# Combine placed one unit later, the first decays in single banks, silu behind the next query's copy, the last products of up and the first banks of down reordered

## The chip, the cores and the metric

The kernel runs on one core of a Trainium2 chip. The metric is the device time of the whole kernel in microseconds (us). The time before is the median of three executions. Its five engines, by the names used here, are TensorE (PE, with its weight loads listed apart as PEld), VectorE (DVE), ScalarE (ACT), GpSimd (POOL) and SyncE (SP), which issues the transfers.

## The reference

Two residual layers over a sequence of 1024 tokens with 1024 features. Layer 0 mixes tokens with a gated MLP and with dilated attention, layer 1 with chunked gated linear attention (GLA); each layer ends with a gated MLP with a causal convolution. Cut to what the change touches:

```python
def even_mixer(h, w_in, a_ln_g, a_ln_b, a_ws, a_bs, q_g, k_g, w_out):
    ...
    for window, dilation in B_BRANCHES:
        o_r, l_r = dilated_branch(qh, kh, vh, window, dilation)
        outs.append(o_r)
        lses.append(l_r)
    wts = jax.nn.softmax(jnp.stack(lses), axis=0)
    o = jnp.einsum('rbhs,rbhsc->bhsc', wts, jnp.stack(outs))
    ...

def gla_mixer(h, w_in, w_a2, b_a, head_g, w_out):
    ...
    log_a = jax.nn.log_sigmoid((ga @ w_a2 + b_a).astype(jnp.float32)) / C_TAU
    o = gla_chunked(heads(q, C_DK) * (C_DK ** -0.5), heads(k, C_DK), heads(v, C_DV),
                    heads(log_a, C_DK))
    o = rms_norm(o, head_g)
    o = o.transpose(0, 2, 1, 3).reshape(Bn, S, hv) * jax.nn.silu(r.astype(jnp.float32))
    return o.astype(h.dtype) @ w_out

def conv_ffn(h, w_gate, w_up, conv_w, conv_b, w_down):
    g = causal_dwconv(h @ w_gate, conv_w, conv_b)
    return (jax.nn.silu(g) * (h @ w_up)) @ w_down
```

## The kernel before

All large products are made in float32 split into a high and a low part, so that each product of two tiles is three matmuls. A split is a copy to the high part (mostly ACT, line 100) and a subtraction for the low part (DVE, line 101). Independent instructions are put in order by the framework's scheduler when the program is built; an instruction that the program hands to `keep_in_program_order` stays where the code has it on its engine. Each engine runs its instructions strictly in that order.

**Attention of layer 0** (`project`, `unit`, `dilated`, `combine`) goes over four pairs of heads. For a pair, `project` makes eight token tiles n: a projection into one of two banks named pj (line 190), a norm of queries and keys (the tile qn, line 768, which is the last reader of pj and lets the bank go), a split of qn on POOL and DVE (qs, ks), transposes, and one `unit` of banded attention (scores sc, mask and sum sm on DVE at line 711, transposes pP, output po). `dilated` then does the strided branch and writes its result to memory (od); it is loaded back in two halves as the tiles on. `combine` weighs the two branches of one half g: a minimum cM (line 838, kept in program order), exponentials cE, and in `combined` the denominators cD and the products at lines 849 to 857, one of them on POOL. While the next pair is projected, the combine of the pair before runs behind two of its units, through the argument `then`.

**GLA of layer 1.** `values` makes the value projections (pv, tag mm, three tiles of two banks each) with the preparation of the decays of head 0 inserted (`decays(0, ...)`, whose two products are the tiles pla, read by ACT and by DVE at line 1083). Then the streams q0, r0, q1, r1, ... follow, one for queries and keys of a head and one for its gate. Each is two of 128-wide row blocks made with seven products numbered 1 to 7 instead of eight; products 1, 6, 7, 4 share a bank B, 5 and 3 share C, 2 has A. The bank of each B product is read before the next one may start: line 1059 copies product 6 (ACT), line 1063 adds product 7 (DVE). After a gate stream, silu is applied to its result `or` in two halves (line 1168, ACT, with a load of the function table ahead of them), and it is written to memory; `core` runs the chunked recurrence (pat, pog, og).

**The MLP.** `ffn_up` works in streams as well, a gate stream g and an up stream u for every two row blocks; the products come as 5, 6, 2, 7, then 1 of the next stream, then 4 and 3. Line 302 copies product 7 (ACT, s1), line 305 product 4. `ffn_down` accumulates over all row blocks into banks named pd: B (two double tiles, pdB and pdC), O (a double tile pdO and the single ones pdP and pdQ). In layer 1 the first product goes to B.

Of the kernel before, what the change touches and what calls it, by code (L numbers as in the profile page):

```python
# [9 lines left out]
F32 = mybir.dt.float32  # L10
# [3 lines left out]
AF = mybir.ActivationFunctionType  # L14
# [5 lines left out]
P = 128  # L20
# [8 lines left out]
HEADS_C = 4  # L29
EPS = 1e-6  # L30
BIG = 1e30
HALVES = ((0, slice(0, 512)), (1, slice(512, 1024)))
# [7 lines left out]
PASSES = ((0, 0), (0, 1), (1, 0))  # L40
# [15 lines left out]
def trunk(ctx: ExitStack, tc: tile.TileContext, a, out):  # L56
# [181 lines left out]
    def ffn_up(l, T3, ps, pool, norm_end):  # L238
# [6 lines left out]
        def stream(kind, f):  # L245
# [31 lines left out]

            def step(p):
                if p not in made:
# [8 lines left out]
                for j in range(4):  # L288
                    for ii, jj in PASSES:
                        T.matmul(o, L[ii][:, j * P : j * P + P], right[p][:, jj, j, :], skip_group_check=more,  # L290
                                 start=(not more and j == 0 and (ii, jj) == PASSES[0]),
                                 stop=(j == 3 and (ii, jj) == PASSES[-1]))
                if p == 1:
# [66 lines left out]
        for i, (kind, f) in enumerate(todo):  # L360
            step, out, _ = cur
            early = (1, 2) if i < 2 else (1,)
            for p in (5, 6, 2, 7):
                if p not in early:
                    step(p)
            if 0 < i < len(todo) - 1:
                nxt = stream(*todo[i + 1])
                nxt[0](1)
            step(4)
            step(3)  # L370
            if kind == "g":
                ts = conv(f, out)
            else:
                for j in range(2):
                    V.tensor_mul(ts[j], ts[j], out[:, j, :])
                down_acts(f, *ts)
                down_weights(f)
            cur = nxt


    def ffn_down(l, ps, pool, xs, final):
# [12 lines left out]
        def mm(o, t, side, start, stop, more):  # L394
            L, R = side
            for ii, jj in PASSES:
# [297 lines left out]
    def attention(ps, at, av, pq, pq0, par0, wx, wq0, gqk, masks, rest, gm_open):  # L694
# [42 lines left out]
        def outputs(name):  # L737
            return (at.tile([P, 4, 132], F32, tag="ot", name="ot" + name, bufs=5),
                    ps.tile([P, 4, P], F32, tag="po", name="po" + name))

        def project(p, ws=None, then=None, early=None):
# [35 lines left out]
            for n in range(NT):  # L777
# [83 lines left out]
        for p in range(PAIRS):  # L861
# [11 lines left out]
            def then(g):  # L873
                weights(g)()
# [23 lines left out]
    def gla(ps, narrow, gl, T3, rl):  # L898
# [43 lines left out]
        def values():  # L942

            for i, (col, step, w) in enumerate(((0, 272, 1), (256, 256, 2), (512, 512, 1))):
# [6 lines left out]
                for m in sorted(range(NT // (2 * w)), key=lambda m: 2 * w * m < 4):  # L951
# [191 lines left out]

        cur = begin(*todo[0])
        cur[0](1)
        for i, (kind, h) in enumerate(todo):
            step, out = cur
            for p in (5, 6, 2, 7) if i + 1 < len(todo) else (6, 2, 7):
                step(p)
            if i + 1 < len(todo):  # L1150
                nxt = begin(*todo[i + 1])
                nxt[0](1)
# [4 lines left out]
            if kind == "q":  # L1157
# [6 lines left out]
                if h + 1 < HEADS_C:  # L1164
                    dc = decays(h + 1)
            else:
                for _, c in HALVES:
                    A.activation(out[:, :, c], out[:, :, c], AF.Silu)
# [177 lines left out]
```

## Time and profile before

| what | value |
|---|---|
| executions | 2165.72, 2161.59, 2159.29 us, median 2161.59 us |
| profiled execution | 2167.37 us, of which the span is 2165.6 us |
| PE busy | 2134.3 us of the span (99%) |
| DVE, ACT, POOL busy | 71%, 48%, 23% of the span |
| mean granted clock of PE | 0.996 |

The profile shows one execution, the profiled one, which is 5.8 us above the median of the others. In the rows, the first number is the start in us from the beginning of the span, the second the duration in us, then come the engine, the line of the code, the operation, what it writes and reads, shape and count of like instructions in a row; a bracket at the end is the idle time of that engine ahead of it and what ended it. Rows of the list of waits give total, times and the longest, in us. Rows by windows give for a stretch of time the busy time of each engine, then the granted clock of PE as a share of full speed, the share of transfers and their rate.

### The profile page before, as it was taken

To read this page: it belongs to the slowest core of one execution; us is meant where nothing else is said; L and a number is where in the kernel's file an instruction comes from. 1 tells how busy PE (TensorE), PEld (TensorE's weight loads), DVE (VectorE), ACT (ScalarE), POOL (GpSimd) and SP (SyncE) were. 2 spreads that over 40 slices of the span, in tenths; PEclk is the share of its full clock that TensorE was granted. 3 is DMA by queue.
4 is the path that set the end of the run, shared out by engine and by line. 5 is a ranking of instruction groups with operands and counts; after the bars stand their busy time and mean duration, and the time that the engine had idled before them with its cause. 6 is when DMAs were issued, how large, how long until landed. Compare 5 with 4: busy or idle time off the path is not lost.

```text
span 2165.6 us, 29712 instructions
## 1 busy us (share of the span) xinstructions
PE 2134.3 (99%) x10444; PEld 1808.8 (84%) x10444; DVE 1530.0 (71%) x2451; ACT 1035.0 (48%) x1998; POOL 491.0 (23%) x521
## 2 busy tenths in 40 slices
PE   8999999999999999999999999999999999999999
PEld 7999988888888888878889888888788888888887
DVE  7566655577888878755577777667788878885554
ACT  7445555354444445444454455534544444444443
POOL 6444411012433424000010011110233425320000
PEclk9999999999999999999999999999999999999999
DMA  7022312664444444675554223386554444457664
GB/s 271 25 72 67 106 40 78 228 220 170 161 168 153 151 160 161 225 255 190 197 195 132 69 98 101 122 293 228 185 166 160 157 151 154 164 180 277 217 216 166
DMA packets 159413, 353.70 MB, mean 163 GB/s; under 512 B 17392, under 2 KB 54256, under 8 KB 158880
## 3 DMA queue, kind: packets, MB, share of 16 engines
q1 hardware_dynamic: 159264, 351.81, 47.6%
q8 instruction: 82, 1.34, 0.2%
q14 instruction: 67, 0.55, 0.1%
HBM read 243.15 MB, written 108.59 MB: 162 GB/s over the span
## 4 chain that ended last, share of the span: by engine, by line
PE 88%; DMA 5%; DVE 3%; ACT 3%; issue 1%; SPq 0%; POOL 0%; ACTq 0%; DVEq 0%
PE puB L290 11%; PE pgB L290 11%; PE pv L190 6%; PE pj L190 6%; PE pgC L290 6%; PE puC L290 6%; PE pdB L397 5%; PE pdC L397 5%; PE po L190 5%; PE pdO L397 4%; PE puA L290 3%; PE pgA L290 3%; PE pdP L397 2%; PE pdQ L397 2%; PE pu L190 2%; PE pBq L1051 2%
## 5 line engine op out<-in xcount | busy, mean ns | idle before, releaser
L101 DVE TENSOR_TENSOR da<-ar,da 128x512 fp32r<-128x512 f32 x154 | 106.3, 690 | 153.4 <-ACT da L100 153.2
L100 ACT CAST da<-ar 128x512 fp32r<-128x512 f32 x154 | 95.9, 623 | 206.9 <-PE pdC L397 97.5
L190 PE MATMUL po<-wo,hq 128*128 128x512 f32 x768 | 184.9, 395 | 2.0 <-ACT hq L100 1.8
L190 PEld LDWEIGHTS po<-wo,hq 128*128 128x128 f32 x768 | 141.3, 188 | 32.9 <-ACT hq L100 2.5
L190 PE MATMUL pv<-wv,hq 128*128 128x512 f32 (+2 forms) x768 | 140.7, 340 | 1.6 <-DVE b L1083 1.6
L397 PE MATMUL pdB<-dw,da 128*128 128x512 f32 x528 | 135.5, 391 | 1.5 <-ACT dw L100 0.8
L397 PE MATMUL pdC<-dw,da 128*128 128x512 f32 x528 | 135.1, 390 | 0.0
L190 PEld LDWEIGHTS pv<-wv,hq 128*128 128x128 f32 x768 | 118.7, 189 | 16.4 <-DVE b L1083 2.1
L397 PEld LDWEIGHTS pdB<-dw,da 128*128 128x128 f32 x528 | 98.7, 188 | 22.9 <-ACT dw L100 1.2
L256 POOL TENSOR_TENSOR S1g<-rg 128x512 f32<-128x512 f32 x20 | 30.7, 1536 | 383.0 <-DMA wsd<-D 325.8
L190 PE MATMUL pj<-wq,hq 128*128 128x384 f32 x576 | 114.7, 348 | 2.7 <-DVE qn L768 2.7
L397 PEld LDWEIGHTS pdC<-dw,da 128*128 128x128 f32 x528 | 99.0, 188 | 20.5
L101 DVE TENSOR_TENSOR dw<-wr,dw 128x512 fp32r<-128x512 f32 x154 | 105.8, 687 | 13.1 <-ACT dw L100 12.9
L140 POOL TENSOR_SCALAR rn<-ssq 128x1 f32<-128x1 f32 x24 | 8.1, 339 | 453.2 <-ACT h L148 246.0
L190 PEld LDWEIGHTS pj<-wq,hq 128*128 128x128 f32 x576 | 103.4, 195 | 3.0 <-DVE qn L768 3.0
L100 ACT CAST dw<-wr 128x512 fp32r<-128x512 f32 x154 | 95.0, 617 | 17.3 <-DMA wr<-in_w_dn 9.5
L397 PE MATMUL pdO<-dw,da 128*128 128x512 f32 x396 | 102.2, 389 | 0.2 <-DVE dw L101 0.2
L397 PEld LDWEIGHTS pdO<-dw,da 128*128 128x128 f32 x396 | 74.3, 188 | 16.0 <-DVE dw L101 0.6
L319 DVE SCALAR_TENSOR_TENSOR t<-g,cw,t 128x1022 f32<-128x1022 f32 x44 | 76.6, 1742 | 0.1
L318 DVE SCALAR_TENSOR_TENSOR t<-g,cw,t 128x1023 f32<-128x1023 f32 x44 | 60.2, 1367 | 16.2 <-ACT t L317 16.2
L303 DVE TENSOR_TENSOR g<-g,s1g 128x512 f32<-128x512 f32 x22 | 16.2, 737 | 77.2 <-ACT s1g L302 77.2
L320 ACT ACTIVATE t<-t 128x1024 f32<-128x1024 f32 x44 | 46.7, 1061 | 32.2 <-DVE t L319 32.2
(1080 smaller groups left out, 5448.3 us busy)
## 6 DMA issues: line engine op xcount, KB each, us to landing
ar<-actd SPq DMA_DIRECT2D x70, 512.0 KB, 3.6
rd<-in_w_down SPq DMA_DIRECT2D x44, 512.0 KB, 3.6
wsd<-D SPq DMA_DIRECT2D x88, 256.0 KB, 2.4
rg<-in_w_gate SPq DMA_DIRECT2D x42, 512.0 KB, 3.5
ru<-in_w_up SPq DMA_DIRECT2D x42, 512.0 KB, 4.5
wr<-wsd SPq DMA_DIRECT2D x40, 512.0 KB, 4.5
actd<-t SPq DMA_DIRECT2D x66, 256.0 KB, 2.1
wr<-in_w_dn SPq DMA_DIRECT2D x30, 512.0 KB, 4.8
```

The lines of the kernel that those rows point to most:

```text
L100: (hi or A.copy)(dst[0], src)
L101: (lo or V.tensor_sub)(dst[1], src, f32(dst[0]))
L140: G.tensor_scalar(r, ssq, 1.0 / n, EPS, op0=ALU.mult, op1=ALU.add)
L190: T.matmul(o, L[i], R[jj][:, sl], start=(k == 0 and (ii, jj) == PASSES[0]), stop=(k == nk - 1 and (ii, jj) == PASSES[-1]))
L256: G.tensor_tensor(sums[name], x, y, op=op)
L290: T.matmul(o, L[ii][:, j * P : j * P + P], right[p][:, jj, j, :], skip_group_check=more, start=(not more and j == 0 and (ii, jj) == PASSES ...
L303: V.tensor_add(C22, C22, s1)
L318: V.scalar_tensor_tensor(t[:, 1:], g[:, : S - 1], w(1), t[:, 1:], op0=ALU.mult, op1=ALU.add)
L319: V.scalar_tensor_tensor(t[:, 2:], g[:, : S - 2], w(0), t[:, 2:], op0=ALU.mult, op1=ALU.add)
L320: A.activation(t, t, AF.Silu)
L397: T.matmul(o, L[ii][:, t * P : t * P + P], R[jj], skip_group_check=more, start=start and not more and (ii, jj) == PASSES[0], stop=stop and ...
L1051: T.matmul(o, L[ii][:, j * P : j * P + P], right[p][:, jj, j, :], skip_group_check=more, start=(not more and j == 0 and (ii, jj) == PASSES ...
```

## The change

`then` runs behind units 4 and 5 instead of 3 and 4, and the tiles ot have six buffers instead of five. The decays of head 0 take their two products pla from single banks (tag pt) instead of double tiles. The silu of a gate stream is issued by the new `gates`, whose two halves are kept in program order, and for all but the last gate only after product 6 of the next query stream. In the first and the last stream of `ffn_up`, product 3 comes ahead of 4 and its first matmul is kept in program order. In layer 1 `ffn_down` takes pdP, pdQ and the tile pdB as bank B, and pdC and pdO as O.

```diff
             if 0 < i < len(todo) - 1:
                 nxt = stream(*todo[i + 1])
                 nxt[0](1)
-            step(4)
-            step(3)
+                step(4)
+                step(3)
+            else:
+                step(3, pin=True)
+                step(4)
...
-        bank = {"B": [w[:, i, :] for w in wide[:2] for i in range(2)],
-                "O": [wide[2][:, i, :] for i in range(2)] + [ps.tile([P, 512], F32, tag="pt", name=f"pd{i}") for i in "PQ"]}
+        single = [ps.tile([P, 512], F32, tag="pt", name=f"pd{i}") for i in "PQ"]
+        halves = [w[:, i, :] for w in wide for i in range(2)]
+        bank = {"B": single + halves[:2], "O": halves[2:]} if l else {"B": halves[:4], "O": halves[4:] + single}
...
-            return (at.tile([P, 4, 132], F32, tag="ot", name="ot" + name, bufs=5),
+            return (at.tile([P, 4, 132], F32, tag="ot", name="ot" + name, bufs=6),
...
-                if then and n in (3, 4):
-                    then(n - 3)
+                if then and n in (4, 5):
+                    then(n - 4)
...
-                        first = decays(0, "mm")
+                        first = decays(0, "pt")
...
+        def gates(h, out):
+            for _, c in HALVES:
+                tc.keep_in_program_order(A.activation(out[:, :, c], out[:, :, c], AF.Silu))
+            if h + 1 < HEADS_C:
+                Q.dma_start(rsd[:, 2 * h : 2 * h + 2, :], out)
...
             for p in (5, 6, 2, 7) if i + 1 < len(todo) else (6, 2, 7):
                 step(p)
+                if p == 6 and pending:
+                    gates(*pending)
+                    pending = None
...
+            elif h + 1 < HEADS_C:
+                pending = h, out
             else:
-                for _, c in HALVES:
-                    A.activation(out[:, :, c], out[:, :, c], AF.Silu)
-                if h + 1 < HEADS_C:
-                    Q.dma_start(rsd[:, 2 * h : 2 * h + 2, :], out)
-                else:
-                    return ps, out
+                gates(h, out)
+                return ps, out
```

Line numbers after the change are six higher in the attention and about sixteen lower at the silu. DVE at the first combine, in the projection of the second pair, before:

```order
L711 ISA sm1n_1697,ot1n_1691<-sc1n_1694,mband 128x4x64
L711 ISA ot1n_1691 128x1
L838 TENSOR_TENSOR cM_1620<-ot0n_624,on_1270 128x8
L711 ISA sm1n_1705,ot1n_1691<-sc1n_1702,mband 128x4x64
L711 ISA ot1n_1691 128x1
L768 SCALAR_TENSOR_TENSOR qn_1835<-pj_1810,r_84,rq_1842 128x256
L841 TENSOR_TENSOR cE_1622<-cM_1620,ot0n_624 128x8
L841 TENSOR_TENSOR cE_1622<-cM_1620,on_1270 128x8
L798 CAST kT_1307<-tk_1781 128x16x32
L768 SCALAR_TENSOR_TENSOR qn_1913<-pj_1888,r_84,rq_1920 128x256
```

The same place after the change:

```order
L717 ISA sm1n_1689,ot1n_1675<-sc1n_1686,mband 128x4x64
L717 ISA ot1n_1675 128x1
L774 SCALAR_TENSOR_TENSOR qn_1835<-pj_1810,r_84,rq_1842 128x256
L804 CAST kT_1307<-tk_1765 128x16x32
L774 SCALAR_TENSOR_TENSOR qn_1913<-pj_1888,r_84,rq_1920 128x256
L101 TENSOR_TENSOR qs_1847<-qn_1835,qs_1847 128x2x64
L101 TENSOR_TENSOR ks_1848<-qn_1835,ks_1848 128x2x128
L101 TENSOR_TENSOR qs_1925<-qn_1913,qs_1925 128x2x64
L737 COPY pT1n_1694<-pP1n_1677 128x512
L844 TENSOR_TENSOR cM_1700<-ot0n_624,on_1270 128x8
```

The minimum cM of the first half stood ahead of both qn; now it stands behind both, and behind the split of the first and half of that of the second. The combine of the second half follows it five instructions later, so that the two run interleaved.

ACT at the silu of the second gate stream (r1), around the copy of query stream q2, before:

```order
L100 CAST wr2p_12916<-S6r_12914 128x512
L1168 ACT_TABLE_LOAD
L1168 ACTIVATE or_12165<-or_12165 128x2x512
L100 CAST wr2p_12932<-rr_12630 128x512
L1168 ACTIVATE or_12165<-or_12165 128x2x512
L1059 COPY oq_12502<-pBq_12507 128x512
L100 CAST wr2p_12951<-S7r_12949 128x512
```

The same place after the change:

```order
L100 CAST wr2p_12916<-S6r_12914 128x512
L100 CAST wr2p_12932<-rr_12630 128x512
L1065 COPY oq_12502<-pBq_12507 128x512
L1152 ACT_TABLE_LOAD
L1152 ACTIVATE or_12165<-or_12165 128x2x512 x2
L100 CAST wr2p_12951<-S7r_12949 128x512
```

The copy of product 6 has moved ahead of the table load and the two silus; the cast for weights wr2p from S7r still stands behind them.

PE where the last up stream of layer 1 meets the first product of down, before:

```order
L290 MATMUL puA_17701<-hq_87,wu20p_17698 128x512 x12
L290 MATMUL puC_17666<-hq_88,wu20p_17752 128x512 x12
L290 MATMUL puB_17603<-T_13976,wu20p_17717 128x512 x12
L290 MATMUL puB_17603<-hq_86,wu20p_17734 128x512 x12
L397 MATMUL pdB<-dw_17843,da_17840 128x512 x6
```

The same place after the change:

```order
L290 MATMUL puB_17603<-T_13976,wu20p_17717 128x512 x12
L290 MATMUL puC_17666<-hq_88,wu20p_17736 128x512 x12
L402 MATMUL pdP<-dw_17843,da_17840 128x512 x3
L402 MATMUL pdQ<-dw_17843,da_17840 128x512 x3
L402 MATMUL pdP<-dw_17849,da_17846 128x512 x3
L402 MATMUL pdQ<-dw_17849,da_17846 128x512
L290 MATMUL puB_17603<-hq_86,wu20p_17752 128x512 x12
L402 MATMUL pdQ<-dw_17849,da_17846 128x512 x2
```

Between product 7 (from T) and product 4 (from hq_86) into the one bank puB there was nothing; now product 3 and ten matmuls of down stand there.

More of the change, by code (lines that the diff above doesn't have):

```diff
@@ L276, in prep, with step @@
                     made[p] = parts_of(left(p), f"w{kind}{f}p{p}")
-            def step(p):
+            def step(p, pin=False):
                 if p not in made:
@@ L289, in step @@
                     for ii, jj in PASSES:
-                        T.matmul(o, L[ii][:, j * P : j * P + P], right[p][:, jj, j, :], skip_group_check=more,
-                                 start=(not more and j == 0 and (ii, jj) == PASSES[0]),
-                                 stop=(j == 3 and (ii, jj) == PASSES[-1]))
+                        mm = T.matmul(o, L[ii][:, j * P : j * P + P], right[p][:, jj, j, :], skip_group_check=more,
+                                      start=(not more and j == 0 and (ii, jj) == PASSES[0]),
+                                      stop=(j == 3 and (ii, jj) == PASSES[-1]))
+                        if pin and j == 0 and (ii, jj) == PASSES[0]:
+                            tc.keep_in_program_order(mm)
                 if p == 1:
@@ L1142, in begin @@
             return stream(f"r{h}", [a["w_r"][2 * h + i] for i in range(2)], rl, tag="r")
-        cur = begin(*todo[0])
+        def gates(h, out):
[3 more added lines that the diff above has]
+                Q.dma_start(rsd[:, 2 * h : 2 * h + 2, :], out)
+        cur, pending = begin(*todo[0]), None
         cur[0](1)
```

## The prediction, on record before the changed kernel ran

> **What bounds the kernel now.** I read the page's summary first, to see which engine the time belongs to.
>
> ```profile
> span 2165.6 us, 29712 instructions
> PE 2134.3 (99%) x10444; PEld 1808.8 (84%) x10444; DVE 1530.0 (71%) x2451; ACT 1035.0 (48%) x1998; POOL 491.0 (23%) x521
> ```
>
> PE is busy for 2134.3 of 2165.6 us. The change removes no matmul and adds none, so it can only win what PE loses: idle time, at most 2165.6 − 2134.3 = 31.3 us, and time in which PE is busy but slow. The second view is therefore the list of PE's waits:
>
> ```profile
> PE pj L190 <- ACT wx L105: 5.7, 1, 5.7
> PE pj L190 <- DVE qn L768: 4.9, 2, 2.7
> PE pBq L1051 <- ACT oq L1059: 2.1, 2, 1.1
> ...
> PE pv L190 <- DVE b L1083: 1.6, 1, 1.6
> PE puB L290 <- ACT s1u L302: 1.4, 2, 0.7
> ...
> PE pdB L397 <- ACT u L305: 0.7, 1, 0.7
> ```
>
> The longest is the start of the program, which the change leaves alone. The other five rows are the places that the change touches, in its five parts, and come to 4.9 + 2.1 + 1.6 + 1.4 + 0.7 = 10.7 us. That is the ceiling of what can be had from idle time in these places.
>
> **Part 1, combine one unit later.** Timelines of DVE (first four rows) and of PE around the two waits of pj:
>
> ```profile
> 125.14 0.17 DVE L838 TENSOR_TENSOR cM<-ot0n,on 128x8 f32<-128x8 f32 x1 [2.18 <-DMA on<-od]
> ...
> 125.77 0.49 DVE L768 SCALAR_TENSOR_TENSOR qn<-pj,r,rq 128x256 f32<-128x256 f32 x1
> ...
> 193.75 0.17 DVE L838 TENSOR_TENSOR cM<-ot1n,on 128x8 f32<-128x8 f32 x1 [2.41 <-DMA on<-od]
> ...
> 194.76 0.48 DVE L768 SCALAR_TENSOR_TENSOR qn<-pj,r,rq 128x256 f32<-128x256 f32 x1
> ```
>
> ```profile
> 126.32 3.82 PE L190 MATMUL pj<-wx,hq 128*128 128x384 f32 x12 [2.13 <-DVE qn L768]
> ...
> 195.29 6.28 PE L190 MATMUL pj<-wq,hq 128*128 128x384 f32 x19 [2.74 <-DVE qn L768]
> ```
>
> DVE stands 2.18 and 2.41 us at cM until on has come from memory; qn is queued behind it, and PE cannot start the next projection until qn has read its bank. After the change both qn stand ahead of cM, and so does a copy of pP that PE makes only behind 19 matmuls of the next projection. By then on has landed, which was 2.2 to 2.4 us after DVE first asked for it. So the two waits, 2.13 + 2.74 = 4.9 us, go. What follows them is visible only by windows:
>
> ```profile
> 121.00:123.50 2.50, 2.50 (x26) 2.50 (x25) 1.64 (x5) 2.24 (x9) 0.44 (x1) 1.00 0.32 77
> 126.30:129.50 3.20, 3.18 (x10) 3.19 (x11) 3.10 (x11) 0.57 (x4) 2.54 (x5) 0.50 0.31 91
> 195.20:201.40 6.20, 6.11 (x19) 6.11 (x20) 5.30 (x14) 0.65 (x4) 4.94 (x7) 0.51 0.19 56
> 1183.40:1189.00 5.60, 5.60 (x25) 4.63 (x26) 1.22 (x2) 5.54 (x6) 0.00 (x0) 1.00 0.14 54
> ```
>
> Ahead of the first wait the granted clock is 1.00; behind the waits of 2.1 and 2.7 us it is 0.50 and 0.51, for at least 3.2 and 6.2 us. Behind the wait of 1.63 us at 1183.38 it is 1.00. So at the two places PE is busy but slow: 10 matmuls in 3.20 us, or 0.32 us each, and 19 in 6.28 us, or 0.33, where 12 of the same shape take 2.24 us, or 0.187, in the next fence. That is 10 x 0.133 + 19 x 0.144 = 4.1 us more, and it goes with the waits. The Trainium skill, page "TensorE: Matmul & The Clock Gate", section "HAM oscillation — how this bites in real kernels", gives as a rule that idle gaps of over about 3.4 us are to be avoided since they throttle the clock to half; by it, waits of 2.1 and 2.7 us would cost only themselves. The windows here show otherwise, and the rule becomes a rival below.
>
> What could give it back is that both combines now run close together on DVE and POOL, ahead of the norms of the tiles after them:
>
> ```profile
> 139.66 2.24 PE L190 MATMUL pj<-wx,hq 128*128 128x384 f32 x12
> ```
>
> ```profile
> 136.71 0.48 DVE L768 SCALAR_TENSOR_TENSOR qn<-pj,r,rq 128x256 f32<-128x256 f32 x1
> 137.11 1.31 DVE L855 TENSOR_TENSOR on<-on,cE 128x512 f32<-128x512 f32 x1
> 138.89 0.69 DVE L857 TENSOR_TENSOR ot0n<-ot0n,on 128x512 f32<-128x512 f32 x1 [0.47 <-DVE on L855]
> ```
>
> ```profile
> 136.83 1.04 POOL L855 TENSOR_TENSOR ot0n<-ot0n,cE 128x512 f32<-128x512 f32 x1 [0.15 <-DVE cE L852]
> ```
>
> Before, qn at 136.71 ends at 137.19 and the projection that needs its bank starts at 139.66: 2.5 us of cover. A half's combine on DVE is 1.31 + 0.69 us for the two large products and about 1.2 us in seven small ones (0.17 to 0.20 each, from the form of cM above), 3.2 us in all, and 1.04 us on POOL. Not all of the second one falls ahead of the next qn: the large products stand behind it in the new order, so it is the small ones, some 1.2 us, against a cover of 2.5. I take nothing as lost here; without cover it would be 3.2 − 2.5 = 0.7 us at each of three pairs, 2.1 us in all. Part 1: −4.9 − 4.1 = **−9.0 us**, bounds −9.0 and, if the clock were not won back and all of the loss came, −4.9 + 2.1 = −2.8.
>
> **Part 2, the first decays in single banks.** PE and DVE:
>
> ```profile
> 1183.38 6.88 PE L190 MATMUL pv<-wv,hq 128*128 128x512 f32 x29 [1.63 <-DVE b L1083]
> ```
>
> ```profile
> 1182.57 1.41 DVE L1083 TENSOR_SCALAR b<-pla,ba 128x512 f32<-128x512 f32 x2 [0.57 <-ACT g L1082]
> ```
>
> The next pv has to wait for the double tiles in which pla sits, until DVE has read them. In single banks pla holds up nobody, as pt has no other user there, and DVE's reading lies beside the 29 matmuls of pv. **−1.6 us**; bound 0 if another bank of pv turns out to be late by as much.
>
> **Part 3, silu behind the query's copy.** Here I follow the chain past the first wait. ACT, DVE and PE at the second gate, and PE and DVE at the third:
>
> ```profile
> 1331.95 1.28 ACT L1168 ACT_TABLE_LOAD   x1
> ...
> 1335.68 0.56 ACT L1059 COPY oq<-pBq 128x512 f32<-128x512 f32 x1
> 1336.14 0.62 ACT L100 CAST wr2p<-S7r 128x512 fp32r<-128x512 f32 x1
> ```
>
> ```profile
> 1336.80 0.69 DVE L101 TENSOR_TENSOR wr2p<-S7r,wr2p 128x512 fp32r<-128x512 f32 x1 [1.26 <-ACT wr2p L100]
> ...
> 1341.26 0.68 DVE L1063 TENSOR_TENSOR oq<-oq,pBq 128x512 f32<-128x512 f32 x1
> ```
>
> ```profile
> 1336.29 3.01 PE L1051 MATMUL pBq<-Tm,wq2p 128*128 128x512 f32 x12 [1.07 <-ACT oq L1059]
> ...
> 1341.99 3.06 PE L1051 MATMUL pBq<-hq,wq2p 128*128 128x512 f32 x12
> ```
>
> ```profile
> 1389.11 3.04 PE L1051 MATMUL pBq<-Tm,wq3p 128*128 128x512 f32 x12 [1.06 <-ACT oq L1059]
> ...
> 1397.20 2.88 PE L1051 MATMUL pBq<-hq,wq3p 128*128 128x512 f32 x12
> ```
>
> ```profile
> 1393.35 0.68 DVE L1063 TENSOR_TENSOR oq<-oq,pBq 128x512 f32<-128x512 f32 x1
> ```
>
> With the copy ahead of the table load, product 7 (pBq from Tm) starts about 1.1 us earlier at both places. But the cast from S7r stays behind load and silus, so its end on ACT does not move. DVE's low part of it starts at 1336.80, and DVE then has seven instructions in a row to line 1063, which ends at 1341.94. Product 4 (pBq from hq) starts at 1341.99, 0.05 us after it. At the second gate, then, the wait only moves from product 7 to product 4. At the third gate line 1063 ends at 1394.03 and product 4 starts at 1397.20, with 3.2 us between: there the 1.06 us stay won. I take **−1.1 us**; bounds 0 and −2.1 (the row of the list of waits).
>
> The last gate's two silus are now kept together, ahead of the last squares of `core`, where before one was done much earlier:
>
> ```profile
> 1422.57 1.06 ACT L1168 ACTIVATE or<-or 128x1024 f32<-128x1024 f32 x1
> ```
>
> ```profile
> 1425.53 4.73 PE L190 MATMUL po<-wo,hq 128*128 128x512 f32 x17 [0.21 <-ACT hq L100]
> ```
>
> PE already waits 0.21 us here for ACT, so a second silu of 1.06 us ahead of it can cost up to that, or nothing, if ACT has as much idle time before hq. I take the middle, **+0.5 us**, bounds 0 and 1.1.
>
> **Part 4, product 3 ahead of 4.** In the last up stream of both layers product 4 waits for the copy of product 7 in the same bank:
>
> ```profile
> 1942.24 2.88 PE L290 MATMUL puC<-hq,wu20p 128*128 128x512 f32 x12
> ...
> 1948.52 3.03 PE L290 MATMUL puB<-hq,wu20p 128*128 128x512 f32 x12 [0.68 <-ACT s1u L302]
> 1952.22 1.66 PE L397 MATMUL pdB<-dw,da 128*128 128x512 f32 x6 [0.68 <-ACT u L305]
> ```
>
> Product 3 (puC, 2.7 us from start to start) now stands between them, four times the wait. Its price is that product 7 runs 2.7 us earlier; its weights lie ready well ahead, since none of the waits names them. **−1.4 us**, bound 0. In the first stream the three last products have no wait in the list, so there the new order is worth nothing.
>
> **Part 5, down's first banks.** The wait at 1952.22 is for the bank that product 4's copy reads. With pdP and pdQ first, ten matmuls of down stand ahead of product 4. **−0.7 us**, bound 0. At the end of the kernel one addition and one store follow the last matmul, in other banks, as before: nothing.
>
> **Sum** against the profiled execution: −9.0 − 1.6 − 1.1 + 0.5 − 1.4 − 0.7 = −13.3, so 2167.4 − 13.3 = 2154.1 us. The median lies 5.8 us below that execution. If other executions lose as much at the half clock, the same 13.3 come off 2161.6: 2148.3. If the half clock (4.1) is what the profiled one had in excess, 9.2 come off: 2152.4. I forecast the middle, **2150.4 us**.
>
> **Rivals.** (a) The half clock belongs to the profiled execution alone. The waits of 4.9 go, the 4.1 are not there to be won in the others, and 2161.6 − 9.2 = 2152.4. For it speaks the scatter of 6.4 us among the three executions; against it that both places in the one trace show the half clock. The same page of the Trainium skill, section "What's actually happening", has the clock watched in windows of 3.4 us that run freely, which speaks for a halving that comes and goes.
> (b) The stall moves. The wait of qn is for on, but the packed combines take its place at 0.7 to 2.1 us per pair, long enough in part to bring the half clock again, and Part 3 gives nothing: −4.9 of Part 1 remain, −1.6, −1.4, −0.7, and +0.5, +2.1: 2161.6 − 6.0 = 2155.6, no measurable change.
> (c) The other side: DVE and POOL together push the next qn beyond its cover. Both halves' POOL product (2 x 1.04) and all DVE work of one half (3.2) would come ahead of it, 5.3 us against 2.5 of cover: an idle time of 2.8 us, as long as the one at 195.29, with 2.7 us lost at the half clock behind it, at each of three pairs, 3 x 5.5 = 16.5. With the 13.3 of the sum taken off, 3.2 us are lost: 2164.8. Without any cover it is 3 x 8.0 = 24 us, and 2161.6 + 24 − 13.3 = 2172.3. It decides where qn slips by more than 2.5 us. Against it stands the new order: the large products lie behind qn.
> (d) The gain of Part 3 comes whole, another −1.0: 2149.4.
>
> **How the numbers follow.** About 0.3%, 6.5 us, is what a measurement can tell from no change: faster is below 2155.1, slower above 2168.1. The forecast with (a) and (d), which all lie below 2155, hold 0.70 (0.45, 0.18, 0.07); (b) with its neighbours 0.18; (c) 0.12, of which 0.08 is above 2168 and 0.04 falls within. So faster 0.70, same 0.22, slower 0.08. The likeliest case alone reaches from 2146 (all of the sum, Part 3 whole, 1 us of scatter) to 2154. The range has to reach to (b) with its bounds and half of (c): 2145 to 2161.
>
> **What would show it.** In the changed profile: no wait of pj for qn at pairs two and three, cM without a wait for on, and a granted clock of 1.00 around 124 to 132 and 190 to 198; no wait of pv for b, none of puB for s1u or of pdB for u; at the second gate a wait of product 4 for line 1063 in place of product 7's for the copy, at the third none. I am wrong if a new wait of over 2 us stands anywhere on PE, above all for qn or qs in the projection behind the packed combines.

## The result, and the profile after

The median fell from 2162.92 us (nine executions of the kernel before) to 2156.42 us (nine of the changed one): 6.5 us, a ratio of 0.9972 with a 95% interval of 0.9961 to 0.9983. A second measurement gave 0.9973 (0.9963 to 0.9983). The forecast was 2150.4 us, 11.2 below the median then known. The time lies inside the stated range and the direction is right, but only 58% of the forecast gain came, and the time is above 2155.1, where the prediction let "faster" end: it gave "same" 0.22 and "faster" 0.70.

The page of the changed kernel, its first lines:

```profile
span 2156.7 us, 29705 instructions
PE 2129.6 (99%) x10444; PEld 1807.1 (84%) x10444; DVE 1525.1 (71%) x2451; ACT 1034.8 (48%) x1998; POOL 493.2 (23%) x521
```

The span of the profiled execution went from 2165.6 to 2156.7, by 8.9 us, where the sum forecast 13.3. PE has the same 10444 matmuls and is busy for 4.7 us less, about what the half clock had cost (4.1 us). Its idle time fell only from 31.3 to 27.1 us, though waits of 10.7 us were to go. The list of PE's waits says why:

```profile
PE pj L190 <- ACT wx L105: 5.8, 1, 5.8
PE pCq L1057 <- ACT vend L973: 1.7, 1, 1.7
...
PE pgB L290 <- ACT hq L100: 1.3, 1, 1.3
PE pdP L402 <- ACT dw L100: 1.2, 1, 1.2
PE pBq L1057 <- DVE oq L1069: 1.2, 1, 1.2
PE pc L448 <- DMA cat<-ogd: 1.1, 2, 0.6
...
PE pdB L402 <- DVE xr L427: 0.8, 1, 0.8
```

All the old rows that the prediction quoted are gone but the start (5.8). In their place stand new ones: pCq for vend (1.7), pdP for dw (1.2), pBq for line 1069 (1.2), pc for cat (1.1), pdB for xr (0.8). The first three stand some way behind a place where an old wait was removed, the others where the change put things in a new order.

The first combine, PE and then DVE, in their timelines:

```profile
123.52 0.41 PE L732 MATMUL pP1n<-ident,sm1n 128*128 128x128 f32 x2
123.69 2.35 PE L190 MATMUL pj<-wx,hq 128*128 128x384 f32 x12
125.88 1.38 PE L190 MATMUL pj<-wq,hq 128*128 128x384 f32 x7
```

```profile
124.61 0.48 DVE L774 SCALAR_TENSOR_TENSOR qn<-pj,r,rq 128x256 f32<-128x256 f32 x1 [0.20 <-ACT vN L767]
128.97 0.15 DVE L844 TENSOR_TENSOR cM<-ot0n,on 128x8 f32<-128x8 f32 x1
130.10 0.16 DVE L844 TENSOR_TENSOR cM<-ot0n,on 128x8 f32<-128x8 f32 x1
132.65 0.48 DVE L774 SCALAR_TENSOR_TENSOR qn<-pj,r,rq 128x256 f32<-128x256 f32 x1
```

Neither pj nor cM has a bracket: PE goes from the transposes into the projection without a wait, and both minima find their data. The qn behind the packed combines ends at 133.13, and the projection that needs its bank starts at 135.52: the cover is 2.4 us, as before. By windows (granted clock third from the end) the half clock is gone at both places:

```profile
125.00:128.00 3.00, 3.00 (x23) 3.00 (x22) 1.64 (x4) 0.00 (x0) 1.60 (x4) 1.00 0.55 134
185.00:191.00 6.00, 6.00 (x49) 5.96 (x49) 4.84 (x13) 3.68 (x13) 3.37 (x7) 1.00 0.54 147
```

The first matmul of the output projection of layer 0, before and after, shows what this stage won, 380.50 − 370.60 = 9.9 us against 9.0 forecast:

```profile
380.50 0.73 PE L190 MATMUL po<-wo,hq 128*128 128x512 f32 x2 [0.96 <-ACT hq L100]
```

```profile
370.60 0.73 PE L190 MATMUL po<-wo,hq 128*128 128x512 f32 x2 [0.96 <-ACT hq L100]
```

So all of the gain, and 1 us more than the whole 8.9, was there at 370 us; the other 1786 us of the program lost a little, where 4.3 were to be won. That 9.9 comes so close to 9.0 is in part luck of the execution. Another execution of the kernel before (the first experiment below), with the half clock at one of the two places, reaches the same matmul at

```profile
375.71 0.73 PE L190 MATMUL po<-wo,hq 128*128 128x512 f32 x2 [0.96 <-ACT hq L100]
```

Against it the changed kernel is 5.1 us ahead here and 2159.5 − 2156.7 = 2.8 us at the end: both say that the rest lost, and the size of part 1 has to be taken from the times.

### The profile page after: what moved, and what is told of

It reads as the page before. It is cut to its first block, busy times and chain, and to the rows that moved or that the text cites. A ratio compares the mean times of both kernels' runs of the same rounds, so it can differ in the third digit from the quotient of the medians.

```text
span 2156.7 us, 29705 instructions
## 1 busy us (share of the span) xinstructions
PE 2129.6 (99%) x10444; PEld 1807.1 (84%) x10444; DVE 1525.1 (71%) x2451; ACT 1034.8 (48%) x1998; POOL 493.2 (23%) x521
## 4 chain that ended last, share of the span: by engine, by line
PE 89%; DVE 4%; DMA 3%; ACT 2%; issue 1%; SPq 0%; POOL 0%; ACTq 0%; DVEq 0%
PE pgB L290 11%; PE puB L290 11%; PE po L190 6%; PE pj L190 6%; PE puC L290 6%; PE pgC L290 6%; PE pv L190 5%; PE pdB L402 4%; PE pdC L402 4%; PE pdO L402 4%; PE puA L290 3%; PE pgA L290 3%; PE pdP L402 2%; PE pdQ L402 2%; PE pu L190 2%; PE pBr L1057 2%
## 5 line engine op out<-in xcount | busy, mean ns | idle before, releaser
L402 PE MATMUL pdC<-dw,da 128*128 128x512 f32 x462 | 119.5, 390 | 0.3 <-DVE dw L101 0.3
L402 PEld LDWEIGHTS pdC<-dw,da 128*128 128x128 f32 x462 | 86.6, 188 | 18.5 <-DVE dw L101 0.7
L402 PE MATMUL pdP<-dw,da 128*128 128x512 f32 x231 | 65.8, 390 | 1.2 <-ACT dw L100 1.2
```

What stands on the lines that cost most here:

```text
L402: T.matmul(o, L[ii][:, t * P : t * P + P], R[jj], skip_group_check=more, start=start and not more and (ii, jj) == PASSES[0], stop=stop and ...
```

## The experiments

Fifteen runs follow, two of them of the unchanged kernels before and after, each beside executions of the kernel before on the same chip. Ratios are to the kernel before, with 95% intervals; three of the runs are single executions and have no ratio.

**The kernel before once more**, unchanged.

> The kernel before once more, to see the granted clock of each execution. Theory G (the missing gain was given back to new waits of PE): the clock of the kernel before is about the same in all executions, 0.996 to 0.997, since both waits of pj for qn bring the half clock each time, and the time of an execution hardly depends on it. Theory C (the half clock is not there in all executions): the clock differs from execution to execution, between 0.996 and 0.999, and the time falls by about 2.1 us for each 0.001, so that the usual execution has only a part of the 4 us to win.

Ratio 1.000 (0.9992 to 1.0009). Of its eleven executions the seven with a mean clock of 0.998 took 2161.3 to 2163.4 us, the four with 0.995 or 0.996 took 2164.6 to 2167.4. The profiled one had 0.998, with waits of pj for qn of 2.4 and 2.8 us. By windows behind the one and the other:

```profile
122.80:126.00 3.20, 3.16 (x18) 3.16 (x19) 3.10 (x11) 0.59 (x4) 2.52 (x5) 1.00 0.23 67
190.30:196.50 6.20, 6.13 (x19) 6.13 (x20) 5.28 (x14) 0.62 (x4) 4.93 (x7) 0.50 0.19 56
```

18 matmuls in 3.20 us behind the first, where the execution of the prediction had 10. The half clock is there in some executions and not in others, which is theory C's picture for the scatter: at the same place a wait of 2.1 us led to it in the profile before (0.50) and a wait of 2.4 us did not in this one (1.00). The Trainium skill, "TensorE: Matmul & The Clock Gate", section "What's actually happening", has a window that runs freely; the two executions agree with it, while its idle time of a whole window, about 3.4 us, is not what the traces show, since 2.8 us sufficed here and 2.1 us in the profile before.

**Part 1 alone.**

```diff
-            return (at.tile([P, 4, 132], F32, tag="ot", name="ot" + name, bufs=5),
+            return (at.tile([P, 4, 132], F32, tag="ot", name="ot" + name, bufs=6),
...
-                if then and n in (3, 4):
-                    then(n - 3)
+                if then and n in (4, 5):
+                    then(n - 4)
```

> The kernel before with part 1 alone. Theory G: 9 us in the profile up to the output projection of layer 0, and as the parts 2 to 5 then gave back as much as they won, the median is 6 to 9 us below that of before, at or below that of the whole change. Theory C: 5 to 6 us, 1 to 3 us less than all parts together.

2154.03 us, 0.9955 (0.9942 to 0.9969): 9.4 us below the median of before, a little more than theory G's 6 to 9: all that the whole change won and some 3 us more. By the medians, then, the other four parts together did not win 4.3 us but lost; the two intervals still overlap (0.9961 to 0.9969).

**The whole change without part 5.**

```diff
-        single = [ps.tile([P, 512], F32, tag="pt", name=f"pd{i}") for i in "PQ"]
...
-        bank = {"B": single + halves[:2], "O": halves[2:]} if l else {"B": halves[:4], "O": halves[4:] + single}
+        bank = {"B": [w[:, i, :] for w in wide[:2] for i in range(2)],
+                "O": [wide[2][:, i, :] for i in range(2)] + [ps.tile([P, 512], F32, tag="pt", name=f"pd{i}") for i in "PQ"]}
```

> The whole change without part 5: down's first banks in layer 1 as before. Theory G: the waits of pdP for dw (1.22 us) and of the last pdB for xr (0.78 us) go, that of pdB for u (0.7 us) does not come back or does, so the span is 1 to 2 us shorter than with part 5. Rival: the wait for dw belongs to the earlier transfers of xr ahead of those of ar and stays with the old banks; then only the last 0.9 us go.

2153.25 us, 0.9955 (0.9942 to 0.9967). In its trace the waits of pdP for dw and of pdB for xr are gone, and that of pdB for u is back:

```profile
PE pdB L402 <- ACT u L307: 0.7, 1, 0.7
```

The stretch in which part 5 acts can be timed in every trace, from the start of product puA in the last up stream to the end of the span. The two starts are, in the changed kernel and in this run:

```profile
1929.37 2.88 PE L290 MATMUL puA<-hq,wu20p 128*128 128x512 f32 x12
```

```profile
1930.54 2.88 PE L290 MATMUL puA<-hq,wu20p 128*128 128x512 f32 x12
```

That is 2156.7 − 1929.37 = 227.3 us with part 5 and 2155.7 − 1930.54 = 225.2 us without it. Five more traces with parts 4 and 5 as in the change have 227.1 to 227.5, two more with part 4 and without part 5 have 225.1 and 225.7. So part 5 costs about 2 us in this stretch, clear of the scatter there. The ratios differ by 0.0017, or 3.7 us; where the rest of that is, if it is more than scatter, no run shows.

**Parts 1 and 5 alone**: the first diff above and part 5's lines on the kernel before.

> The kernel before with parts 1 and 5 alone. If part 5 itself loses, new waits of pdP for dw (1 us or more) and of the last pdB for xr (0.8 us) are there, and the ratio is 0.9960 to 0.9975, above that of part 1 alone (0.9955). Rival: it loses only together with part 4; then there is no wait of pdP for dw and the ratio is at or below 0.9955.

2157.70 us, 0.9975 (0.9966 to 0.9984), against 0.9955 for part 1 alone: part 5 by itself takes about 0.0020 or 4.3 us (the two intervals touch at 0.9966 to 0.9969). Its list of waits has what does it:

```profile
PE pdP L397 <- ACT dw L100: 2.2, 1, 2.2
```

With the last pdB for xr (0.78) and one of pdC for dw (0.31) that is 3.3 us of waits, and the wait of pdB for u (0.68) is not even gone there. What goes instead is the wait of product 4 for s1u in layer 1 (0.68), as down's matmuls now stand ahead of it, so 2.6 us net. The stretch from the last puA (1924.95) to the end of the span takes 229.4 us, where it is 226.1 with part 1 alone: 3.2 us more. This is what was expected if part 5 itself loses.

**Parts 1 and 4 alone**: the first diff above and, in `ffn_up`, product 3 ahead of 4.

> The kernel before with parts 1 and 4 alone. Theory: both waits of puB for s1u (0.7 us each) go and nothing takes their place, 1.4 to 1.7 us below part 1 alone, a ratio of 0.9945 to 0.9955. Rival: down's first chunk in layer 0 or the way of product 4 through memory takes it back; then a wait of pdB for dw grows by 0.7 us and the ratio is 0.9955 or above.

2154.70 us, 0.9959 (0.9946 to 0.9973). Both waits of puB for s1u are gone from the trace, as the theory had it, but the ratio and a wait for dw are the rival's. But at about 921 us, behind the first of the two places, down's first chunk of layer 0 waits 0.58 us for dw. This wait was 0.82 us in the profile before and under 0.1 in the three other traces without part 4 (the kernel before once more, part 1 alone, parts 1 and 5); in the thirteen traces with part 4 it is always there, 0.14 to 0.98 us, 0.56 on average. So some of the gain in layer 0 is given back to this chunk, and what is left of 1.4 us is too small to be seen in these times.

**The whole change once more.**

> The whole change once more, beside the two below on one chip. If part 5 is what the change lost against its first part, it stays at a ratio of 0.997; if its first measurement was a chance, it comes out at 0.9955 like the runs without part 5.

2156.43 us, 0.9973 (0.9963 to 0.9983): no chance.

**Banks in turn.** The last wait, seen in the changed kernel's PE:

```profile
2145.03 3.56 PE L402 MATMUL pdB<-dw,da 128*128 128x512 f32 x15
2149.37 3.70 PE L402 MATMUL pdB<-dw,da 128*128 128x512 f32 x15 [0.78 <-DVE xr L427]
```

Before, pdB and pdC took turns here, without a wait:

```profile
2155.00 3.56 PE L397 MATMUL pdB<-dw,da 128*128 128x512 f32 x15
2158.40 3.56 PE L397 MATMUL pdC<-dw,da 128*128 128x512 f32 x15
```

Now the two halves of the one tile pdB come last and one behind the other.

```diff
-        bank = {"B": single + halves[:2], "O": halves[2:]} if l else {"B": halves[:4], "O": halves[4:] + single}
+        bank = {"B": [single[0], halves[0], single[1], halves[1]], "O": halves[2:]} if l else {"B": halves[:4], "O": halves[4:] + single}
```

> The whole change with part 5's banks in turn: pdP, first half of pdB, pdQ, second half of pdB. If the last wait (0.78 us, for DVE's read of the other half of the same tile) comes from two halves of one tile used one after the other, it goes, and 0.9 us with it; the wait of pdP for dw stays at 1.2. If it comes from the addition or the store itself, it stays at 0.8 in another place.

The wait is gone and that of pdP for dw stays at 1.1, as expected: the order of the halves made it. From the last puA to the end it is 226.2 us, 1.1 less than in the changed kernel. The time, 2157.92 us or 0.9972 (0.9961 to 0.9984), does not show this.

**Product 4 kept ahead of down**, on the banks in turn.

```diff
-                step(4)
+                step(4, pin=i > 0)
...
-                T.matmul(o, L[ii][:, t * P : t * P + P], R[jj], skip_group_check=more,
...
+                prod = T.matmul(o, L[ii][:, t * P : t * P + P], R[jj], skip_group_check=more,
...
+                if l and start and (ii, jj) == PASSES[0] and not pinned:
+                    pinned.append(tc.keep_in_program_order(prod))
```

> Part 5 with its banks in turn, and product 4 of the last up stream kept ahead of down's first matmuls. If the wait of pdP for dw (1.1 to 1.2 us) comes from product 4's being 2.3 us later, since its result goes to memory and back before down's last chunk can be cast, then it falls to under 0.4 us, and the wait of pdB for u does not come back: 1 to 2 us less than with the banks in turn alone. Rival: the loads of xr delay the chunk; then the wait stays at 1 us or more.

0.9983 (0.9969 to 0.9996), the slowest of all. The wait of pdP for dw grew to 3.5 us and came earlier. ACT in this run:

```profile
1961.96 0.62 ACT L100 CAST dw<-wr 128x512 fp32r<-128x512 f32 x1 [10.37 <-DMA wr<-in_w_dn]
```

ACT stands for weights that have nothing to do with product 4; their load was issued at 1951.00, behind eight loads of xr of 512 KB each (from 1946.01 on). So the wait did not fall to 0.4 us, and my theory of product 4's way through memory does not explain it; the rival does: the chunk is late because of xr. In the changed kernel the transfers over the same stretch, by windows (share of transfers next to last):

```profile
1950.00:1960.00 10.00, 10.00 (x46) 8.29 (x45) 4.67 (x7) 4.15 (x7) 0.00 (x0) 1.00 1.04 385
1960.00:1967.00 7.00, 7.00 (x33) 5.79 (x32) 0.00 (x0) 0.00 (x0) 0.00 (x0) 1.00 1.03 404
```

The transfer engines are full for 17 us, 385 to 404 GB/s. ACT and DVE do nothing at all from 1960 to 1967: they wait for data. The load of ar for the late chunk (256 KB, issued at 1957.06 behind those of xr) takes 10.3 us to land, where the median of the loads of ar of this size is 2.9. In the profile before the same loads filled the engines too (1.02 from 1970 to 1977), and no wait of PE followed: there was slack, and part 5 uses it up.

**xr late**: the eight loads of xr issued behind those of down's last chunk, on the banks in turn.

```diff
-        for n in range(NT):
-            Q.dma_start(xs[n], xd[l][n])
+        def load_x():
+            for n in range(NT):
+                Q.dma_start(xs[n], xd[l][n])
+
+        if not l:
+            load_x()
...
+                if l and p == 1 and i == len(CHUNKS) - 1:
+                    load_x()
```

> Part 5 with its banks in turn, and the eight loads of xr issued behind the loads for down's last chunk instead of two loads ahead of them. If the block of xr loads (4 MB) makes that chunk's casts late, the wait of pdP for dw (1.1 us with the banks in turn, 3.5 with product 4 first) goes to under 0.3 us, and none for xr takes its place. If the way of product 4's result through memory is what is late, it stays at 0.8 us or more.

0.9968 (0.9956 to 0.9981). The wait of pdP is gone, but two of pdC of 0.95 and 0.81 us stand at the next chunk, whose loads now lie behind xr: only four of the eight were moved by the scheduler past one pair of loads. So xr's 4 MB take their place in a stretch that is full of transfers, and what is behind them waits. This is half a confirmation: xr is the cause of the wait at its old place, but moving it only moved the wait, and the stretch from the last puA to the end is 226.5 us, no shorter than with the banks in turn alone (226.2).

**The last gate as before.**

```diff
-                gates(h, out)
+                for _, c in HALVES:
+                    A.activation(out[:, :, c], out[:, :, c], AF.Silu)
                 return ps, out
```

In the changed kernel, PE at the start of layer 1's output projection:

```profile
1412.36 0.73 PE L190 MATMUL po<-wo,hq 128*128 128x512 f32 x2 [0.53 <-ACT hq L100]
1413.51 0.96 PE L190 MATMUL po<-wo,hq 128*128 128x512 f32 x3 [0.42 <-DVE hq L101]
1415.08 0.87 PE L448 MATMUL pc<-ident,cat 128*128 128x128 f32 x4 [0.60 <-DMA cat<-ogd]
```

```profile
1415.50:1420.00 4.50, 4.50 (x16) 3.62 (x15) 2.60 (x6) 1.63 (x3) 0.00 (x0) 0.64 1.02 332
```

PE waits three times within 3.5 us for 1.55 us, and behind that the granted clock is 0.64, where the profile before had one wait of 0.21 here and a clock of 1.00 (1425 to 1432).

> The whole change, but the last gate's two silus as before, not kept together. If they cause the new waits at the start of layer 1's output projection, the waits of po for hq (0.53 and 0.42 us) and of pc for cat (0.57 to 0.79 us) at about 1412 to 1416 us go, 0.2 us for hq stays, the half clock behind them goes, and the span is 1.5 to 3 us shorter. Rival: the waits come from the order of pc and po and the load of cat, which the scheduler chose for another reason; then at least 1 us of them stays.

0.9963 (0.9944 to 0.9981), not to be told from the whole change. The trace gives the answer, PE at the same place:

```profile
1413.65 4.74 PE L190 MATMUL po<-wo,hq 128*128 128x512 f32 x17 [0.21 <-ACT hq L100]
```

The three waits are one of 0.21 us again, as before the change. Keeping both silus together, at a moment when ACT had squares and casts to do, made them: the three waits stand in all nine traces of kernels that keep them together, and in none of the eight others. The lower clock behind them does not always come. The 19 matmuls of po behind the third wait, in the changed kernel and with the banks in turn:

```profile
1415.60 6.06 PE L190 MATMUL po<-wo,hq 128*128 128x512 f32 x19
```

```profile
1416.37 4.59 PE L190 MATMUL po<-wo,hq 128*128 128x512 f32 x19
```

In three of the nine traces they take 5.7 to 6.1 us, in the other six 4.6. The span of this run's trace, 2156.4 us, is 0.3 shorter than that of the changed kernel; the 1.5 to 3 us that were expected do not show in it.

**The decays in double tiles again.**

```diff
-                        first = decays(0, "pt")
+                        first = decays(0, "mm")
```

> The whole change without part 2. If ACT's and DVE's work between the values and the first query stream sets the pace there, the wait of pv for b (1.6 us) comes back and that of pCq for vend (1.7 us) goes, and PE reaches the first pCq and all behind it at the same time as with part 2, within 0.4 us. Rival: part 2 is worth something; then the stream starts 1 us or more later.

PE in this run and in the changed kernel:

```profile
1171.94 32.91 PE L190 MATMUL pv<-wv,hq 128*128 128x512 f32 x144 [1.63 <-DVE b L1089]
1204.69 2.89 PE L1057 MATMUL pBq<-hq,wq0p 128*128 128x512 f32 x12
1207.41 2.94 PE L1057 MATMUL pCq<-Tm,wq0p 128*128 128x512 f32 x12
```

```profile
1202.35 2.88 PE L1057 MATMUL pBq<-hq,wq0p 128*128 128x512 f32 x12
1206.97 3.02 PE L1057 MATMUL pCq<-Tm,wq0p 128*128 128x512 f32 x12 [1.74 <-ACT vend L973]
```

The wait of pv is back and that of pCq is gone. Counted from a matmul that both have behind down's first chunk of layer 0 (924.83 and 924.34 us), pCq starts 282.58 us later in this run and 282.63 in the changed kernel: in this pair of single executions part 2 wins nothing (the time of this one is 2157.52 us). ACT's copies of vend, which free the bank of pCq, stand behind seven casts of weights for the first streams, and these keep their time.

**The weights for product 7 of the gate stream ahead of the silus.**

```diff
                 nxt = begin(*todo[i + 1])
                 nxt[0](1)
+                if pending:
+                    nxt[0].prep(7)
+                    gates(*pending)
+                    pending = None
```

> The whole change, but the gate stream's weights for product 7 (from S7r) are cast ahead of table load and silus. If the wait of product 4 (1.2 us, for DVE's line 1069) comes from DVE standing 3.5 us for this cast, it goes at about 1330 us, and no wait of pBq is left there. Rival: line 1069 is late because of DVE's other work; then at least 0.6 us of it stays.

One execution, 2158.1 us, and not a test of what it was meant for: with the silus called later in the code, the scheduler put the copy of product 6 behind them again, and product 7 waits 1.6 and 1.2 us for that copy. No wait of product 4 is left, but product 7's own would hide it.

**The low part of those weights on GpSimd.**

```diff
-                L = parts_of(left(p), f"w{name}p{p}")
+                if p == 7 and name[0] == "r":
+                    w7 = wp.tile([P, 2, 512], F32R, tag="w", name=f"w{name}p{p}")
+                    L = [w7[:, i, :] for i in range(2)]
+                    split(L, left(p), lo=lambda o, x, h: G.tensor_tensor(o, x, h, op=ALU.subtract))
+                else:
+                    L = parts_of(left(p), f"w{name}p{p}")
```

> The whole change, but the low part of the gate stream's weights for product 7 is made on GpSimd, so that DVE no longer stands 3.5 us for the cast from S7r. If that stand makes line 1069 late, the wait of product 4 (1.2 us at about 1330 us) goes, with no wait of 0.5 us or more of pBq or pBr in its place. Rival: DVE's own seven instructions are what is late; then at least 0.6 us of it stays.

The wait of product 4 grew, from 1.20 to 1.69 us, in one execution of 2158.4 us. PE and DVE:

```profile
1330.45 3.04 PE L1062 MATMUL pBq<-hq,wq2p 128*128 128x512 f32 x12 [1.69 <-DVE oq L1074]
```

```profile
1325.90 0.88 DVE L101 TENSOR_TENSOR wq3p<-rq,wq3p 128x512 fp32r<-128x512 f32 x1 [4.54 <-ACT wq3p L100]
1326.71 0.68 DVE L1034 TENSOR_TENSOR S3r<-rr,S6r 128x512 f32<-128x512 f32 x1
```

DVE no longer stands for the cast from S7r. It stands 4.5 us for the next one, wq3p, which lies behind the same silus and ends 1 us later. So the cause is not that one cast but the order: whatever DVE has next needs a cast that ACT makes behind table load and silus, and line 1074 (1069 in the changed kernel) is queued behind it.

**All mended**, with the four edits of the last gate, the banks in turn, xr late and the low part, and **mended with the old banks**, the last gate and the low part without part 5.

> The whole change with the last gate as before, the banks in turn, xr late and the low part on GpSimd. If the four places are what was given back, PE's waits at 1330, 1412 to 1416, 1968 and 2149 us are gone together, 5 to 6 us of the span against the whole change, so a ratio to before of 0.994 to 0.996. Rival: waits move elsewhere and the ratio stays at 0.997.

> The same mends, but without part 5 (and so without the banks in turn and xr late). Theory: the wait of pdB for u (0.7 us) is back and the rest gone, the ratio to before 0.994 to 0.996, within 0.001 of the run with all mended.

0.9963 (0.9951 to 0.9975) and 0.9954 (0.9941 to 0.9967; 2154.72 us). With part 5 mended, waits of pdC of 1.24 and 0.55 us remain; without part 5 that of pdB for u alone. These are the waits of `ffn_down` in layer 1. At 1330 us nothing was mended: the low part on GpSimd had just been seen to make the wait longer, and both runs have it so, the first one here:

```profile
1331.78 3.06 PE L1068 MATMUL pBq<-hq,wq2p 128*128 128x512 f32 x12 [1.69 <-DVE oq L1080]
```

So the waits at the four places did not go together, and the first theory's 0.994 to 0.996 was missed by a little; what the three useful mends are worth without the fourth was not run. No mended version is better than part 1 alone by more than these intervals tell. The four kernels without part 5 have 0.9954 to 0.9959, the eight measurements with it (two of them of the changed kernel) 0.9963 to 0.9983: no kernel of one group lies among the other.

## Why the prediction was right about part 1 and wrong about the rest

The sum had −9.0 us for part 1 and −4.3 for the other four. Part 1 came as forecast; the others, by the medians, lost some 3 us. The step that failed by most is part 5, "−0.7 us, bound 0": it put the price of ten matmuls ahead of product 4, and of new last banks, at nothing, and the runs show a loss of 2 to 3 us in its stretch of the traces and of 3.7 to 4.3 by the times. The second is part 2, −1.6, which is 0.

- **Part 1** was forecast at 9.0 us and measured at 9.4 alone (interval 6.7 to 12.5). The mechanism holds in each step: qn ahead of cM, no wait for on, no half clock, 2.4 us of cover for the packed combines. Rival (c) fell. Rival (a) was right in its mechanism: the half clock comes in some executions only, so part of its 4.1 us is not there in the usual one. The forecast's middle between the two was a choice and not a reckoning, and that 9.4 lies so near to 9.0, in so wide an interval, is partly luck. Rival (b) counts the loss without cover at "0.7 to 2.1 us per pair", where part 1 had 0.7 per pair and 2.1 in all; its sum uses the latter, and the traces show none.
- **Part 2**, forecast −1.6, is 0. The step that failed is "the next pv has to wait for the double tiles" taken as the end: I gave "bound 0 if another bank of pv turns out to be late by as much" and did not follow the chain to the next bank. It was pCq's, held by vend, and late by 1.7.
- **Part 3**, −1.1: the chain was right. At the second gate the wait moved to product 4 for line 1069 (1.20), at the third none is left. From the first pCq of the streams to the first po of layer 1 PE takes 206.5 to 206.7 us in the five traces without part 3 and 205.1 in the one that has it with the last gate as before, so 1.4 us were won. My named cause for the wait that is left, the cast from S7r, was too narrow. The **last gate**, forecast at +0.5 with a bound of 1.1, cost 1.55 − 0.21 = 1.3 us of waits and, in three traces of nine, a stretch at a lower clock; the bound was of one instruction, and the squares, casts and the load of cat queued behind it were not counted.
- **Part 4**, −1.4: both waits are gone, as forecast; part of it is given back in layer 0 to a chunk whose wait of 0.82 us I had not listed. In layer 1, from the last puA to the end, 226.1 us became 225.1 to 225.7.
- **Part 5**, forecast −0.7, is the step that failed by most: +1.2 + 0.3 + 0.8 of new waits against 0.7 won in the changed kernel, and, with part 1 and without part 4, about +4.3 us by the times. "At the end of the kernel one addition and one store follow the last matmul, in other banks, as before: nothing" was wrong, since the two last sums now come out of two halves of one tile (shown by the banks in turn). And the ten matmuls of down ahead of product 4 were priced by PE alone. Nothing was said of the transfers in this stretch, 4 MB of xr besides the loads of down, which fill it to a share of 1.03; with so little slack, a chunk that PE reaches earlier, or whose data are stored later, is waited for. That xr's loads make the wait is shown by where it went when they moved. Whether PE's arriving 0.8 us sooner or product 4's being later uses up the slack is not fully separated, as the run that was to tell them apart moved xr as well. Counted from the start of product 7, PE comes to the chunk at 35.5 us in the seven traces with parts 4 and 5 and xr at its old place and order, and at 36.3 to 36.5 in the three with part 4 and without part 5. The cast of the chunk's da starts at 35.2 to 35.5 in the former, and at 33.8, 34.0 and 35.2 in the latter. So PE's being sooner is there in every trace and would by itself have made a wait in one of the three; that the data are also later because of product 4 is likely and not shown.

## What to carry to other kernels

A wait that is removed is worth only what the next resource in line has to spare: follow the same chain on each engine to the next bank, copy or load that PE will ask for, and take its slack from the trace, before the wait's length is put into a sum. In this kernel, whose bound engine is 99% busy, only part 1's win stands clear of the scatter of the times; those of parts 3 and 4 can be seen in their stretches of the traces, and part 2's was gone 35 us later. Where several parts go into one change, timing the same stretch between two fixed matmuls in many traces told more than the times did: 2 us were clear there that the medians could hardly tell. Reordering that looks free on the busy engine has to be priced on the transfer queue too, wherever the share of transfers is near 1.

## What the runs showed of the hardware that was not expected

The granted clock also fell without any single wait of 2 us: three waits of 0.53, 0.42 and 0.60 us within 3.5 us were followed by 0.64 in the changed kernel, while a wait of 1.63 us at 1183 us in the kernel before, with PE busy on both sides, was followed by 1.00. But the length of a wait does not decide it alone. The same three waits were followed by the full speed in six traces of nine, and a single wait of 2.23 us (parts 1 and 5 alone, 1966 us) by 1.00, where waits of 2.13 and 2.79 us had led to 0.50 in other executions and one of 3.54 us (product 4 kept ahead) to 0.72 over the next 6 us.

Some of the scatter between executions of one kernel comes from here. In the eleven executions of the kernel before once more, the medians at clocks of 0.998 and of 0.995 to 0.996 lie 4 us apart; with all the executions of it beside the other runs taken in, 44 and 16 with these clocks, they lie 2.4 us apart (2163.3 and 2165.7), and the two groups overlap.
